# Which blocks are multiplied by seven products instead of eight, and in which order a pair's chunks run

## The chip, the core and the metric

The kernel runs on one core of one Trainium2 chip. The metric is the time of one execution on the device, in microseconds. Three runs of the kernel before took 2064.39, 2067.76 and 2068.39 us; the median, 2067.76 us, is the time before. The engines are called TensorE (PE in the profile), VectorE (DVE), ScalarE (ACT), GpSimd (POOL) and SyncE (SP, which issues the DMA transfers).

## The reference, cut to what matters

Two layers, each on 256 tokens of 2048 channels in float32. A layer normalises its input, multiplies it by one wide matrix, runs three kinds of attention on the result, and merges them:

```python
for l in range(DEPTH):
    h = rmsnorm(x, pre_norm_g[l])
    proj = jnp.einsum('bsd,dn->bsn', h, w_in[l])
    (qa, ka, va, qb, kb, vb, qc, kc, vc, za, zb, zc, gates) = jnp.split(proj, split_points, axis=-1)
    ya = neighbourhood_attention(...)              # branch A
    yb = gqa_attention(...)                        # branch B
    yc = dilated_mixture(...)                      # branch C
    ga, gb, gc = jnp.split(sigmoid(gates + b_gate[l]), 3, axis=-1)
    merged = (ga * ((ya * silu(za)) @ w_branch_a[l]) + gb * ((yb * silu(zb)) @ w_branch_b[l])
              + gc * ((yc * silu(zc)) @ w_branch_c[l]))
    x = x + rmsnorm(merged @ w_out[l], post_norm_g[l])
```

## The kernel before, in words

Nearly all the work is the product of the 256 tokens with streamed weights. Weights come in *blocks* of 512 output columns (`Blk`), and a block in *chunks* of 256 input channels, 512 KB each. One tile of a chunk holds two quarters, 128 input channels by 512 columns each. A chunk goes through four steps. SyncE issues its transfer (`emit_raw`). ScalarE rounds it to a high part (`emit_hi`, line 225). VectorE subtracts that from the weight for a low part (`emit_lo`, line 233). TensorE then makes, for each of the two quarters and each half T of the tokens, three matmuls of 512 columns (`mm3`, lines 188 to 190: high by high, low by high, high by low). A plain chunk is so 2 x 2 x 3 = 12 matmuls, a block of eight chunks 96.

The kernel writes out every engine's order by hand. `stream` lists the chunks, `order` says in which order TensorE works them, and before each step `ahead` emits the preparation of chunks further down the stream: transfers six chunks ahead, high parts three, low parts two. Near a pair (below) it looks further: transfers eight chunks ahead, low parts five, two at a time (`near`, lines 273 to 281). Each engine does its instructions strictly in the order of emission. After each chunk `slot` lets one or two steps of other work in: evacuations of finished blocks from PSUM (`evq`), attention heads (`heavy`), and *turns* (`tr_job`, `turn`). A turn rearranges tokens: VectorE transposes (line 166), SyncE sends the result to memory (line 171), and brings it back in another layout (line 175); ScalarE and VectorE then split it into high and low parts. SyncE issues in order too, so what is queued behind a turn's transfer waits with it.

Some blocks run as a *pair* (`two_blocks`). For the first two chunks of both blocks (a *unit* is one of these chunk pairs, `UNITS` is 2) seven block products stand for eight: with two token halves, two quarters and two blocks, each unit is a two-by-two block product, and the seven products of 128 x 128 x 512 are formed from sums and differences of its parts. The token sums come from `combos` (lines 477 to 491), once per layer for the layer's input (`CH`) and once for the merged tokens (`CM`). The weight differences are made for every unit by four subtractions of 128 x 512 on VectorE (lines 244 to 247, in the profile at line 237 of `minus`). A unit has parts A, B and C of two quarters each and shares a part D with the other unit, so the two units need seven tiles split where four plain chunks need four. The steps s1 to s6 issue the products (42 matmuls in all), interleaved with the first plain chunks; four sums of products are kept in SBUF (`total`, line 345), and one is added to each of the four accumulators when its block is evacuated (`whole`, line 397). From there the two blocks take turns by chunk: first block's chunk 3, second's 3, first's 4, and so on.

A layer's blocks come in this order: the gate path of branch C; its nine blocks of queries, keys and values (one plain, then four pairs); branch A, eight plain blocks; branch B, five; four *merges*; four output blocks. A merge has three gate blocks (the first two a pair), then the projections of A, C and B (four, two and four chunks); its result is turned and split (`mt_job`) for the output blocks, whose chunks 2 nb and 2 nb + 1 read the tokens of merge nb. The first two output blocks are a pair, the fourth works its token halves staggered (`lag`).

In the stretch of layer 0 of which the rows speak most: branch C's pairs start at 51.69, 104.06, 146.22 and 188.65 us, the plain blocks of A and B run from 234.99 to 544.54, the merges' gate pairs start at 544.54, 660.71, 755.99 and 847.87, and the output pair runs from 941.17 to 991.88. In layer 1 the merges and the output pair run from 1567.14 to 2016.19.

Of the kernel before, what the change touches and what calls it, by code (L numbers as in the profile page):

```python
# [30 lines left out]
UNITS = 2  # L31


class Blk:


    def __init__(self, w, nk, stat, evac, pre=None):
        self.w, self.nk, self.stat, self.evac, self.pre = w, nk, stat, evac, pre
        self.nc = nk // 2
        self.lag = False  # L40
        self.far = False
        self.twin = None
        self.twinned = False
        self.before = {}
        self.after = {}

# [18 lines left out]
def trunk(ctx, tc, x, xT, wpack, wbr_a, wbr_b, wbr_c, wout, pre_g, qk_g, bgate, post_g, abias,  # L65
# [127 lines left out]
    stream = []  # L193
    st = dict(raw=0, hi=0, lo=0, done=-1)
    RAW, HI, LO = {}, {}, {}
    order, ps = [], {}
# [109 lines left out]
    def two_blocks(one, two):  # L306

        units = [Unit(one, two, kc) for kc in range(UNITS)]
        head = units[0]
        head.all = units  # L310
        j = len(stream)
        for u in units:
            stream.extend([(u, "A"), (u, "B")])
        p1 = len(stream)
        stream.append((one, UNITS))
        stream.extend((u, "C") for u in units)
        d = len(stream)
        stream.append((head, "D"))
        rest = len(stream)
        stream.append((two, UNITS))  # L320
        for kc in range(UNITS + 1, one.nc):
            stream.extend([(one, kc), (two, kc)])
        bank, keep = {}, {}

        def plain(n, T):
            def f(u):
                h, lo, jj = one.stat(u.kc * 2 + n)
                c = slice(T * P, (T + 1) * P)
                return h[:, jj, c], lo[:, jj, c]
            return f  # L330

        def comb(n):
            def f(u):
                t = one.combos[u.kc]
                return t[:, 0, n], t[:, 1, n]
            return f

        def new(*names):
            for n in names:
                bank[n] = mm.tile([P, 512], F32, name="acc")  # L340
            ps.update({(blk, T): bank[n] for n, blk, T in
                       (("a", one, 0), ("d", one, 1), ("c", two, 0), ("w", two, 1)) if n in bank})

        def total(n, x, y):
            nc.vector.tensor_tensor(out=keep[n], in0=x, in1=y, op=ALU.add)  # L345

        def room():
            t = U("keep", [2, 512])
            return t[:, 0], t[:, 1]

        def s1():
            new("p1", "p5")
            product(bank["p1"], units, plain(0, 0), "A", 0, True)
            product(bank["p5"], units, comb(0), "B", 0, True)
            keep["c11"], keep["p16"] = room()
            nc.scalar.copy(keep["c11"], bank.pop("p1"))

        def s2():
            new("a")
            product(bank["a"], units, plain(1, 0), "A", 1, False)  # L360

        def s3():
            new("p6")
            product(bank["p6"], units, comb(1), "B", 1, True)
            total("p16", bank.pop("p6"), keep["c11"])
            for u in units:
                for x in "AB":
                    del u.h[x], u.lo[x]
            st["done"] = p1 - 1

        def s4():
            new("d")
            product(bank["d"], units, plain(1, 1), "C", 1, False)
            keep["c12"], keep["c21"] = room()
            total("c12", bank.pop("p5"), keep["p16"])

        def s5():
            new("p7")
            product(bank["p7"], units, comb(2), "C", 0, True)
            for u in units:  # L380
                del u.h["C"], u.lo["C"]
            st["done"] = d - 1

        def s6():
            new("c")
            product(bank["c"], units, comb(3), "D", 0, False)
            del head.h["D"], head.lo["D"]
            st["done"] = d
            total("c21", bank["p7"], keep["p16"])
            keep["c22"] = keep.pop("p16")  # L390
            total("c22", bank.pop("p7"), keep["c12"])
            new("w")

        def whole(evac, of):
            def f(T, x):
                k = keep.pop(of[T])
                nc.vector.tensor_tensor(out=x, in0=x, in1=k, op=ALU.add)  # L397
                yield from evac(T, x)
            return f

        one.evac, two.evac = whole(one.evac, ("c11", "c21")), whole(two.evac, ("c12", "c22"))

        order.extend([(p1 - 1, s1), (p1, s2), (p1, 0), (p1, s3), (d - 1, s4), (p1, 1), (d, s5), (d, s6),
                      (rest, 0), (rest + 1, 0), (rest, 1), (rest + 1, 1)])
        order.extend((i, T) for i in range(rest + 2, len(stream)) for T in range(2))


    prev = {}
# [1 line left out]
    def layer(l):  # L410
        blocks = []
# [81 lines left out]
        CH, CM = {}, {}  # L493

        def proj(nb, evac, pre=None):
            b = Blk([wpack[l, nb, kc] for kc in range(8)], 16, stat_h, evac, pre)
            b.combos = CH
            blocks.append(b)
            return b
# [277 lines left out]
        def merge(nb):  # L777
            G, BG = {}, {}

            def pre(i):  # L780
                def f():
                    BG[i] = work.tile([P, 512], F32, name="bg", bufs=3)
                    nc.sync.dma_start(out=BG[i], in_=bass.AP(
                        tensor=bgate.tensor, offset=bgate.offset + l * 6144 + i * 2048 + nb * 512,
                        ap=[[0, P], [1, 512]]))
                return f

            def evac_g(i):
                def f(T, ps):
                    if T == 0:  # L790
                        G[i] = U("g", [2, 512])
                    g = G[i][:, T]
                    nc.vector.scalar_tensor_tensor(g, ps, S["rs"][T], BG[i], op0=ALU.mult, op1=ALU.add)  # L793
                    nc.scalar.activation(g, g, AF.Tanh, scale=0.5)  # L794
                    yield
                return f

            def mt_job():

                MT[nb] = pair("mT", [4, 256])  # L800
                return tr_job(MT[nb], G[0])

            def evac_p(i):
                def f(T, ps):
                    nc.vector.scalar_tensor_tensor(G[i][:, T], G[i][:, T], 1.0, ps, op0=ALU.add, op1=ALU.mult)
                    if i:
                        nc.vector.tensor_tensor(out=G[0][:, T], in0=G[0][:, T], in1=G[i][:, T], op=ALU.add)
                    if i == 1 and T == 1:
                        later(mt_job())
                    yield  # L810
                return f

            gs = [proj(23 + 4 * i + nb, evac_g(i), pre=pre(i)) for i in range(3)]
            gs[0].pair(gs[1])
            for i, w, nk, ub in ((0, wbr_a, 8, (("a", 0), ("a", 1))), (2, wbr_c, 4, (("c", 0),)),
                                 (1, wbr_b, 8, (("b", 0), ("b", 1)))):
                blocks.append(Blk([w[l, nb, kc] for kc in range(nk // 2)], nk, stat_y(ub), evac_p(i)))
# [50 lines left out]
        second = cb[0]  # L868
        for k in (1, 3, 5, 7):
            cb[k].pair(cb[k + 1])  # L870
        for kc in range(UNITS):
            second.at("after", (6 + kc, 0), lambda kc=kc: CH.update({kc: combos(stat_h, kc)}))
        a_unit(0)
        a_unit(1)
        b0 = proj(20, evac_z(("b", 0)))
# [5 lines left out]
        for nb in range(4):  # L881
            merge(nb)
        outs = [out_block(nb) for nb in range(4)]
        outs[0].pair(outs[1])
        for kc in range(UNITS):
            blocks[-5].at("after", (1 + kc, 0), lambda kc=kc: CM.update({kc: combos(stat_m, kc)}))
        lastb = outs[3]
        lastb.lag = True

# [28 lines left out]
    for l in range(DEPTH):  # L918
        bl, S = layer(l)
        S0 = S0 or S  # L920
        for b in bl:
            i = len(stream)
            if b.twin:
                two_blocks(b, b.twin)
            elif not b.twinned:
                stream += [(b, kc) for kc in range(b.nc)]
                if b.lag:
                    a = [(i + k, 0) for k in range(b.nc)]
                    c = [(i + k, 1) for k in range(b.nc)]
                    order += a[:LAG]  # L930
                    for k in range(b.nc - LAG):
                        order += [a[LAG + k], c[k]]
                    order += c[b.nc - LAG:]
                else:
                    order += [(i + k, T) for k in range(b.nc) for T in range(2)]
# [3 lines left out]
    for i in range(8):  # L939
        nb, k = divmod(i, 2)  # L940
# [21 lines left out]
    for i, T in order:  # L962
        b, kc = stream[i]
# [119 lines left out]
```

## Time and profile before

| | us |
|---|---|
| median of three runs | 2067.76 (2064.39 to 2068.39) |
| the profiled execution: its own time | 2070.55 |
| the profiled execution: its span | 2068.2 |
| TensorE busy | 2006.3 (97%), 8990 matmuls |
| weight loads of TensorE | 1652.1 (80%) |
| VectorE busy | 1529.8 (74%) |
| ScalarE busy | 1066.4 (52%) |
| mean DMA rate | 226 GB/s |

The span runs from the first instruction of the program to the last; 2.35 us of the execution's own time lie around it. A busy share is the time in which an engine had an instruction running. Matmuls overlap, so the mean duration of one in a row (some 0.39 us) is longer than the time from one start to the next, and a busy TensorE may still be a slow one: the granted clock (PEclk) in a stretch's row tells at which of its two levels, 1.2 or 2.4 GHz, it ran, as a share of the higher.

### The profile page before, as it was taken

What the parts mean: (1) busy time and instruction counts of PE and PEld (TensorE: products, weight loads), DVE (VectorE), ACT (ScalarE), POOL (GpSimd) and SP (SyncE); (2) the same over time, 40 slices, a digit from 0 to 9 for tenths busy, and PEclk for the clock granted to TensorE, in tenths of its full rate; (3) what the DMA queues carried; (4) which work ended last, traced back from release to release, by engine and by line L of the source; (5) the groups of instructions that cost most, each with busy time, mean ns of one, the idle gap of its engine ahead of it and who ended that gap; (6) DMA issues with size and microseconds to landing.
All of it is one profiled execution on the core that took longest, in us unless ns stands there. A gap on an engine that the chain in (4) does not pass through costs nothing.

```text
span 2068.2 us, 24958 instructions
## 1 busy us (share of the span) xinstructions
PE 2006.3 (97%) x8990; PEld 1652.1 (80%) x8990; DVE 1529.8 (74%) x1973; ACT 1066.4 (52%) x1580; POOL 21.5 (1%) x31
## 2 busy tenths in 40 slices
PE   9899999999899999998999999999999999999988
PEld 7787888888677888787888878888887778787876
DVE  6888576768778676758688885876777786757675
ACT  6555465546555445444575554655555644444443
POOL 0000000000000000000000000000000000000000
PEclk9999999999999999999999999999999999999999
DMA  9556576756565647565756674858565657465643
GB/s 341 204 212 251 191 271 254 261 207 250 196 227 222 253 158 261 202 240 186 262 173 237 242 273 154 293 209 324 197 240 192 225 197 265 182 231 211 233 186 138
DMA packets 171724, 468.09 MB, mean 226 GB/s; under 512 B 15440, under 2 KB 58576, under 8 KB 171600
## 3 DMA queue, kind: packets, MB, share of 16 engines
q1 hardware_dynamic: 171600, 466.50, 61.9%
q8 instruction: 70, 1.15, 0.2%
q14 instruction: 54, 0.44, 0.1%
HBM read 427.11 MB, written 39.32 MB: 226 GB/s over the span
## 4 chain that ended last, share of the span: by engine, by line
PE 75%; DVE 13%; DMA 5%; ACT 3%; issue 3%; SPq 0%; DVEq 0%; POOL 0%; ACTq 0%; POOLq 0%
PE acc L189 24%; PE acc L188 24%; PE acc L190 24%; DVE wl L233 3%; DMA raw<-in_wpack_dram 2%; DVE wl L237 2%; DVE tt L166 1%; DMA tx<-turn 1%; DVE ta L237 1%; DVE tb L237 1%; DMA turn<-tt 1%; ACT wh L225 1%; DMA x<-in_x_dram 1%; DVE acc L397 0%; DVE keep L345 0%
## 5 line engine op out<-in xcount | busy, mean ns | idle before, releaser
L189 PE MATMUL acc<-wl,hTh 128*128 128x512 f32 x2080 | 816.5, 393 | 22.4 <-DVE wl L233 11.5
L188 PE MATMUL acc<-wh,hTh 128*128 128x512 f32 x2080 | 817.4, 393 | 3.0 <-DVE s L721 2.7
L190 PE MATMUL acc<-wh,hTl 128*128 128x512 f32 x2080 | 813.7, 391 | 0.0
L233 DVE TENSOR_TENSOR wl<-raw,wh 128x1024 fp32r<-128x1024 f32 (+1 forms) x634 | 751.3, 1212 | 65.3 <-ACT wh L225 63.9
L225 ACT CAST wh<-raw 128x1024 fp32r<-128x1024 f32 (+1 forms) x634 | 633.6, 1041 | 171.8 <-DMA raw<-in_wpack_dram 98.8
L189 PEld LDWEIGHTS acc<-wl,hTh 128*128 128x128 f32 x2080 | 393.2, 189 | 111.4 <-DVE wl L233 16.9
L188 PEld LDWEIGHTS acc<-wh,hTh 128*128 128x128 f32 x2080 | 393.2, 189 | 85.3 <-issue 3.5
L190 PEld LDWEIGHTS acc<-wh,hTl 128*128 128x128 f32 x2080 | 392.8, 189 | 82.3
L189 PE MATMUL acc<-wl,yTh 128*128 128x512 f32 x320 | 124.8, 390 | 1.2 <-DVE wl L233 1.2
L188 PE MATMUL acc<-wh,yTh 128*128 128x512 f32 x320 | 124.6, 389 | 0.0
L190 PE MATMUL acc<-wh,yTl 128*128 128x512 f32 x320 | 124.5, 389 | 0.0
L397 DVE TENSOR_TENSOR acc<-acc,keep 128x512 f32<-128x512 f32 x72 | 49.8, 692 | 74.9 <-PE acc L190 74.9
L794 ACT ACTIVATE g<-g 128x512 f32<-128x512 f32 x48 | 30.4, 633 | 140.1 <-DVE g L793 140.1
L189 PE MATMUL acc<-wl,mTh 128*128 128x512 f32 x236 | 93.2, 395 | 7.1 <-DVE wl L237 7.1
L257 ACT CAST wh<-ta 128x1024 fp32r<-128x1024 f32 x36 | 37.9, 1053 | 120.3 <-DVE ta L237 117.5
L569 ACT ACTIVATE sp<-sp,nm 128x256 f32<-128x256 f32 (+1 forms) x48 | 27.6, 577 | 131.0 <-DVE nm L564 131.0
L188 PE MATMUL acc<-wh,mTh 128*128 128x512 f32 x236 | 93.6, 397 | 0.0
L190 PE MATMUL acc<-wh,mTl 128*128 128x512 f32 x236 | 92.9, 394 | 0.0
L188 PE MATMUL acc<-wh,cs 128*128 128x512 f32 x144 | 59.9, 416 | 17.6 <-ACT cs L147 10.4
L166 DVE STREAM_TRANSPOSE tt<-tok 128x512 f32<-128x512 f32 (+1 forms) x72 | 72.8, 1049 | 0.0
L793 DVE SCALAR_TENSOR_TENSOR g<-acc,rsx,bg 128x512 f32<-128x512 f32 x48 | 36.0, 749 | 49.2 <-PE acc L190 48.1
L189 PEld LDWEIGHTS acc<-wl,yTh 128*128 128x128 f32 x320 | 60.1, 188 | 14.2 <-DVE wl L233 2.0
(137 smaller groups left out, 1864.9 us busy)
## 6 DMA issues: line engine op xcount, KB each, us to landing
raw<-in_wpack_dram SPq DMA_DIRECT2D x558, 512.0 KB, 6.0
raw<-in_wo_dram SPq DMA_DIRECT2D x64, 512.0 KB, 7.5
turn<-tt SPq DMA_DIRECT2D x50, 512.0 KB, 3.0
tx<-turn SPq DMA_DIRECT2D x50, 512.0 KB, 5.8
raw<-in_wa_dram SPq DMA_DIRECT2D x32, 512.0 KB, 4.3
raw<-in_wb_dram SPq DMA_DIRECT2D x32, 512.0 KB, 3.9
turn<-tt SPq DMA_DIRECT2D x34, 256.0 KB, 2.2
tx<-turn SPq DMA_DIRECT2D x34, 256.0 KB, 4.5
```

The source lines that it names most:

```text
L166: nc.vector.transpose(out=tt[:, :, T].rearrange("p j (h a) -> p h j a", h=n), in_=srcs[T].rearrange("p (h b j) -> p h j b", h=n, j=4))
L188: nc.tensor.matmul(out_, lhsT=lh, rhs=rh, start=first, stop=False)
L189: nc.tensor.matmul(out_, lhsT=lh, rhs=rl, start=False, stop=False)
L190: nc.tensor.matmul(out_, lhsT=ll, rhs=rh, start=False, stop=last)
L225: nc.scalar.copy(HI[i][:, k], RAW[i][:, k])
L233: nc.vector.tensor_tensor(out=LO[i][:, k], in0=RAW[i][:, k], in1=f32(HI[i][:, k]), op=ALU.subtract)
L237: nc.vector.tensor_tensor(out=out_, in0=a, in1=b, op=ALU.subtract)
L257: nc.scalar.copy(u.h[what], RAW[u, what])
L397: nc.vector.tensor_tensor(out=x, in0=x, in1=k, op=ALU.add)
L569: nc.scalar.activation(p[:, i], sc[:, i], AF.Exp, bias=nm[:, i:i + 1], scale=1.0 if f is None else f[:, i:i + 1], accum_out=sm[:, i:i + 1])
L793: nc.vector.scalar_tensor_tensor(g, ps, S["rs"][T], BG[i], op0=ALU.mult, op1=ALU.add)
L794: nc.scalar.activation(g, g, AF.Tanh, scale=0.5)
```

## The change

Three things are edited.

- The merges' gate blocks and the output blocks are no longer pairs; all three gate blocks of a merge run as plain blocks. The four pairs of branch C in each layer stay. The first two output blocks become *mates*: six chunks of the first, six of the second, then the last two of the first and the last two of the second. The token sums of the merged tokens (`CM`) go.
- In a pair that stays, the first block's chunk 3 is put ahead of part D, both token halves of it before s6, and after that the first block's chunks 4 to 7 run before the second's 3 to 7. So the first block's last chunk stands five chunks ahead of the second's (one before). A flag `late` that would run their last two chunks otherwise is never set.
- The two token sums of the layer's input are emitted behind chunks 3 and 4 of the block ahead of the first pair, instead of chunks 6 and 7.

```diff
@@ two_blocks
         stream.append((one, UNITS))
         stream.extend((u, "C") for u in units)
-        d = len(stream)
-        stream.append((head, "D"))
+        mid = len(stream)
+        stream.extend([(one, UNITS + 1), (head, "D")])
+        d = mid + 1
         rest = len(stream)
         stream.append((two, UNITS))
-        for kc in range(UNITS + 1, one.nc):
-            stream.extend([(one, kc), (two, kc)])
+
+        ones, twos = list(range(UNITS + 2, one.nc)), list(range(UNITS + 1, two.nc))
+        if one.late:
+            stream.extend([(one, kc) for kc in ones[:-2]] + [(two, kc) for kc in twos[:-2]])
+            ones, twos = ones[-2:], twos[-2:]
+        stream.extend([(one, kc) for kc in ones] + [(two, kc) for kc in twos])
...
-            st["done"] = d - 1
+            st["done"] = mid - 1
...
-        order.extend([(p1 - 1, s1), (p1, s2), (p1, 0), (p1, s3), (d - 1, s4), (p1, 1), (d, s5), (d, s6),
-                      (rest, 0), (rest + 1, 0), (rest, 1), (rest + 1, 1)])
-        order.extend((i, T) for i in range(rest + 2, len(stream)) for T in range(2))
+        order.extend([(p1 - 1, s1), (p1, s2), (p1, 0), (p1, s3), (mid - 1, s4), (p1, 1), (mid - 1, s5),
+                      (mid, 0), (mid, 1), (d, s6)])
+        order.extend((i, T) for i in range(rest, len(stream)) for T in range(2))
@@ merge
-            gs = [proj(23 + 4 * i + nb, evac_g(i), pre=pre(i)) for i in range(3)]
-            gs[0].pair(gs[1])
+            [proj(23 + 4 * i + nb, evac_g(i), pre=pre(i)) for i in range(3)]
@@ layer
         for kc in range(UNITS):
-            second.at("after", (6 + kc, 0), lambda kc=kc: CH.update({kc: combos(stat_h, kc)}))
+            second.at("after", (3 + kc, 1), lambda kc=kc: CH.update({kc: combos(stat_h, kc)}))
...
-        outs[0].pair(outs[1])
-        for kc in range(UNITS):
-            blocks[-5].at("after", (1 + kc, 0), lambda kc=kc: CM.update({kc: combos(stat_m, kc)}))
+        outs[0].mate, outs[1].mated = outs[1], True
@@ trunk
-            elif not b.twinned:
+            elif b.mate:
+                m = b.mate
+                stream += [(b, kc) for kc in range(6)] + [(m, kc) for kc in range(6)]
+                stream += [(c, kc) for c in (b, m) for kc in range(6, 8)]
+                order += [(k, T) for k in range(i, len(stream)) for T in range(2)]
+            elif not b.twinned and not b.mated:
```

## Rows read from the trace of the kernel before

**Rows 1.** The page: its span, and busy us (share of the span) and instructions of each engine

```profile
span 2068.2 us, 24958 instructions
...
PE 2006.3 (97%) x8990; PEld 1652.1 (80%) x8990; DVE 1529.8 (74%) x1973; ACT 1066.4 (52%) x1580; POOL 21.5 (1%) x31
```

**Rows 2.** Busy us of each engine by stretch; x: instructions; PEclk: granted TensorE clock

```profile
core 0: us, PE busy (x) PEld busy (x) DVE busy (x) ACT busy (x) POOL busy (x), PEclk, DMA share, GB/s
104.06:146.22 42.16, 42.16 (x188) 34.92 (x186) 33.79 (x39) 21.71 (x27) 0.00 (x0) 1.00 0.67 249
234.99:544.54 309.55, 309.55 (x1470) 260.03 (x1468) 226.61 (x314) 172.11 (x290) 6.25 (x8) 1.00 0.65 239
544.54:991.88 447.34, 427.36 (x1880) 349.62 (x1878) 331.09 (x422) 211.15 (x291) 2.02 (x2) 0.98 0.59 215
1567.14:2016.19 449.05, 430.03 (x1879) 351.32 (x1878) 330.96 (x421) 210.80 (x291) 2.02 (x2) 0.98 0.60 214
544.54:602.13 57.59, 51.36 (x229) 40.60 (x228) 45.50 (x78) 31.43 (x69) 2.02 (x2) 0.97 0.60 206
602.13:631.13 29.00, 25.69 (x127) 21.52 (x126) 22.21 (x39) 18.18 (x36) 0.00 (x0) 1.00 0.59 209
660.71:707.03 46.32, 44.08 (x187) 35.99 (x186) 34.73 (x39) 20.87 (x24) 0.00 (x0) 0.96 0.64 238
941.17:991.88 50.71, 45.10 (x188) 36.43 (x186) 37.67 (x46) 21.45 (x26) 0.00 (x0) 0.93 0.49 182
188.65:234.99 46.34, 44.07 (x188) 35.98 (x187) 30.39 (x34) 22.97 (x28) 0.00 (x0) 0.96 0.62 227
1210.62:1257.13 46.51, 43.95 (x187) 35.90 (x186) 30.69 (x35) 22.96 (x28) 0.00 (x0) 0.96 0.62 229
51.69:104.06 52.37, 45.99 (x188) 36.80 (x186) 44.79 (x58) 26.62 (x34) 0.00 (x0) 0.90 0.54 202
```

**Rows 3.** What PE waited for, 544.54 to 991.88 us: total, times, longest

```profile
PE acc L189 <- DVE wl L237: 9.2, 7, 3.5
PE acc L189 <- DVE wl L233: 5.5, 4, 3.3
```

**Rows 4.** PE's timeline, start of the second merge's pair: start us, duration us, instruction

```profile
661.39 0.39 PE L188 MATMUL acc<-wh,hTh 128*128 128x512 f32 x1
664.02 0.67 PE L189 MATMUL acc<-wl,hTh 128*128 128x512 f32 x1 [2.24 <-DVE wl L237]
```

**Rows 5.** Busy time in the stretch just behind that wait

```profile
664.50:667.40 2.90, 2.90 (x8) 2.31 (x7) 2.87 (x4) 1.49 (x3) 0.00 (x0) 0.50 0.06 21
```

**Rows 6.** DVE's groups by line and shape: count | busy us, mean ns | idle before

```profile
L397 DVE TENSOR_TENSOR acc<-acc,keep 128x512 f32<-128x512 f32 x72 | 49.8, 692 | 74.9 <-PE acc L190 74.9
L345 DVE TENSOR_TENSOR keep<-acc,keep 128x512 f32<-128x512 f32 x72 | 49.3, 684 | 0.6
L237 DVE TENSOR_TENSOR wl<-ta,wh 128x1024 fp32r<-128x1024 f32 x36 | 43.8, 1218 | 1.2 <-ACT wh L257 1.2
...
L237 DVE TENSOR_TENSOR ta<-raw 128x512 f32<-128x512 f32 x36 | 24.7, 685 | 3.2 <-DMA raw<-in_wpack_dram 3.1
```

**Rows 7.** PE's timeline in layer 0's last branch C pair

```profile
201.96 0.50 PE L188 MATMUL acc<-wh,cs 128*128 128x512 f32 x1 [2.27 <-DVE keep L345]
```

**Rows 8.** DVE's timeline beside it

```profile
201.23 0.67 DVE L345 TENSOR_TENSOR keep<-acc,keep 128x512 f32<-128x512 f32 x1
```

**Rows 9.** DVE's timeline ahead of the first pair

```profile
38.94 1.23 DVE L233 TENSOR_TENSOR wl<-raw,wh 128x1024 fp32r<-128x1024 f32 x1 [1.09 <-ACT wh L225]
...
56.87 0.68 DVE L554 SCALAR_TENSOR_TENSOR tok<-tok,acc 128x512 f32<-128x512 f32 x1
57.46 1.22 DVE L233 TENSOR_TENSOR wl<-raw,wh 128x1024 fp32r<-128x1024 f32 x1
```

**Rows 10.** SP's own waits, 235 to 544 us, ahead of a turn's transfer

```profile
SPq L171 <- DVE tt L166: 174.8, 22, 15.3
```

**Rows 11.** SP's own waits, 941 to 992 us, ahead of a turn's transfer

```profile
SPq L171 <- DVE tt L166: 23.0, 1, 23.0
```

More of the change, by code (lines that the diff above doesn't have):

```diff
@@ L42, in __init__ @@
         self.twin = None
-        self.twinned = False
+        self.twinned = self.late = self.mated = False
+        self.mate = None
         self.before = {}
```

## The prediction

> **What bounds the kernel now.** I read the busy shares first, then busy time by stretch, then TensorE's waits, then the timelines at the longest of them. The shares make TensorE the bound: 2006.3 of 2068.2 us [rows 1]. So work added there should cost, and the question is what its time is made of.
>
> An undisturbed pair shows the price of a matmul. In 104.06 to 146.22 a seven-product pair issues 186 weight matmuls (42 for products, 12 chunks of 12) in 42.16 us without a gap: 0.2267 us each [rows 2]. The attention stretch, 234.99 to 544.54, holds thirteen plain blocks, 1248 weight matmuls or 282.9 us, and some 221 smaller matmuls in the other 26.6, 0.12 us each. TensorE is busy through all of its 309.55 us there, with VectorE busy for 226.61, 73% [rows 2]. Plain blocks beside heavy head work thus lose nothing.
>
> The stretches from the first merge to the end of the output pair are different. Each holds five of the ten pairs that the change dissolves: 5 x 186 + 4 x 216 = 1794 weight matmuls (406.7 us) and about 85 smaller ones (10.2), 416.9 us of issue. They last 447.34 and 449.05 [rows 2]. So 30.4 and 32.1 us, together 62.5, are lost, of which the table's idle time shows only a part. The rest is clock. TensorE waits for a difference of a prepared unit: at 664.02 a matmul starts 2.63 us after the last instead of 0.23 [rows 4], and right behind it the granted clock is 0.50, that is 1.2 GHz, with eight matmuls in 2.90 us [rows 5]. The wait of 2.24 costs 4.2 us in its pair (46.32 less 42.16) [rows 2].
>
> Where it lies, layer 0: first merge's pair 57.59 less 42.16 and 43 small ones at 0.12, 10.3; the third gate block behind it 29.00 less 21.76 and 31 small ones, 3.5; second merge 4.2; output pair 50.71 less 42.16, 8.6 [rows 2]. The remaining 3.8 are in merges three and four and the last projection of the first. The waits named most are units' differences (9.2 us, line 237) and plain chunks' (5.5, line 233) [rows 3], both VectorE's: it is late although busy for only 331.09 of 447.34 us [rows 2].
>
> **The change part by part.** I add the terms to the profiled execution, 2070.55 us with 2.35 outside its span; the median of the runs shown, 2067.76, lies 2.8 lower.
>
> (a) Products. Ten pairs (four merges and one output pair in each of two layers) go from 42 to 48 matmuls over their first two chunk pairs: 60 x 0.2267 = **+13.6 us**, all on TensorE, which has no cover for it.
>
> The Trainium skill, "TensorE: Matmul & The Clock Gate", section "Back-to-back issue gap", gives N/2.4 + 2.5 ns for a matmul on its own, 215.7 ns at 512 columns, and about 131 ns sustained. By those the sixty would be an estimated 12.9 or 7.9 us; this trace's 226.7 ns decides.
>
> (b) What the pairs cost VectorE. Each drops four differences of a chunk's quarters per unit, eight at 0.69; four totals at 0.68; four additions ahead of evacuation at 0.69; and its units need seven tiles split instead of the plain four, three more at 1.22 [rows 6]. That is 5.5 + 2.7 + 2.8 + 3.7 = 14.7 us per pair, 147 in ten, much of it bunched ahead of the pair's first matmul, plus the output pairs' token sums. ScalarE drops three casts and a copy per pair. Each five-pair stretch would then keep about 331 - 74 = 257 us of VectorE work over 423.7 us, 61%, under the 73% at which the attention stretch lost nothing. In the first merge's three gate blocks it is 45.50 + 22.21 - 14.7 = 53 over some 74, 72%, just that level [rows 2].
>
> So I let the 62.5 us go, but not quite: in the first merge the rotary evacuation of the block before now meets head jobs, in a plain block whose split runs two chunks ahead rather than five. From the attention stretch that costs 0; from the third gate block's 3.5 (a plain-chunk wait) up to 3.5 per layer, or below nothing by no more than rounding since the issue floor holds. I take 1.5 per layer, nearer the attention stretch because of its VectorE share. **-59.5**.
>
> The output pair's new order needs the last merge's turned tokens twelve chunks in, 32.6 us; its job emits the turned split after its sixth chunk. Beginning with six chunks of the first block needs only the three earlier merges' tokens. I cost it at nothing; the cover is those six chunks, 16.3 us, and if the turn were later than that the excess would be a wait.
>
> (c) Branch C's order. The fourth product (D) moves behind both halves of a plain chunk: 12 matmuls, 2.72 us. In the last pair of each layer D waits 2.27 us [rows 7] for the first total, which ends at 201.9 [rows 8]; the two pairs lose 46.34 and 46.51 less 42.16, 4.2 and 4.35 [rows 2]. D would now come at 199.5 + 2.72 = 202.2. The block that ends earlier (four chunks sooner; its partner's end is five chunks behind it) also takes two evacuation additions out of VectorE's queue at the next pair's start, 1.4 us. The chunk moved ahead of D needs its split 1.2 us earlier than D's; it takes D's place in the same queue of six. The second block's other half is no longer interleaved, but starts 1.36 us later than before. Bounds: 0 (the wait moves to that chunk) and 8.55; with both shifts pointing one way I take **-8.4**. The other pairs lose nothing today.
>
> (d) Token sums three chunks earlier. Layer 0's first pair loses 52.37 - 42.16 = 10.2 [rows 2]. VectorE works there without rest from the first units on, so sums put ahead only delay the units behind them. What they gain: the two instructions that today stand before the last sum, the gate path's 0.68 and a plain chunk's 1.22 [rows 9], no longer hold up the first products, and some of the 1.09 us gaps ahead of each split [rows 9] are filled; with fewer half-clock matmuls after a shorter wait I take **-3.5**, between +1 (the last chunk before the pair is now late) and -10.2. Layer 1's first pair has VectorE far ahead; nothing there.
>
> Sum: +13.6 - 59.5 - 8.4 - 3.5 = **-57.8**: 2070.55 would be 2012.8, and 2067.76 gives **2010 us**.
>
> **Rivals.**
> 1. VectorE stays late in the first merge. Then its 10.3 + 3.5 stay in both layers, 24.6 more than the 3 that I left: 2035. For it: evacuations with rotary and heads fall together. Against: same VectorE share as a stretch that loses nothing, and the pair's bunch gone.
> 2. TensorE's work alone counts: the waits belong to VectorE's general lag and come back at other instructions. Then +13.6 meets only (c) and (d), -11.9: 2069, no change. For it: 97% busy. Against: the plain blocks between the pairs. The Trainium skill, "Perfetto Trace Analysis", section "Identifying the Most-Contended Engine", says to optimise first the engine with the highest occupancy, and to judge TensorE by its weight loads; by that rule, adding to TensorE is the wrong way. The weight-load share of 80% shows room, so the trace only half agrees.
> 3. Slower: SP's queue. The merged tokens' turn holds SP until VectorE has transposed; in the output pair that was 23.0 us [rows 11], and weights behind it are not issued. Pairs look eight chunks ahead for transfers, plain blocks six, 16.3 us. Were SP held as long, each of eight starts (merges two to four, the output pair, two layers) would lose 6.7 plus some 1.7 of half clock [rows 5], 67 us against 62.5 - 13.6 + 11.9 = 60.8 gained: 2074. It decides from 7.6 us per start. Against: SP was held up to 15.3 us under the same six chunks in the attention stretch [rows 10], without loss, and VectorE's bunch, which made the 23.0, goes.
> 4. All lost time goes, the first pair's included: 48.9 + 8.6 + 10.2 = 67.7, 2000.
>
> **How the numbers follow.** Forecast (2003 to 2022) 0.76, rival 1 in whole 0.10, rival 2 0.02, rival 3 0.03, rival 4 0.09. The range 2000 to 2030 takes in the bounds of (b) to (d) and half of rival 1. A difference under about 0.2%, 4 us, is no change here: faster 0.95, same 0.02, slower 0.03.
>
> **What would show it.** The two stretches should last about 425 us each, with TensorE's gaps under 2 us and granted clock 1.00; the last branch C pairs 42.2; the first pair some 49, its wait now for a unit's difference and not for a sum. VectorE's busy time should fall by about 155 us, TensorE's count rise by 60. Rival 1 would leave waits for line 233 in the first merge, rival 2 waits spread over the plain blocks, rival 3 ScalarE waiting for transfers with TensorE idle behind it. The prediction is wrong if the two stretches stay above 437.

## The result and the profile after

The changed kernel takes 2017.21 us (median of 4, 2014.5 to 2018.05) against 2068.07 beside it: ratio 0.9753, 95% interval 0.9734 to 0.9771, so 50.9 us faster. The forecast was 2010 within 2000 to 2030. The profiled execution took 2016.78 us, with a span of 2014.7; the steps below are compared by spans, 53.5 us apart.

The page of the changed kernel: span, and busy time by engine [rows 1].

```profile
span 2014.7 us, 24751 instructions
...
PE 1994.3 (99%) x9050; PEld 1651.9 (82%) x9050; DVE 1387.9 (69%) x1749; ACT 1029.2 (51%) x1526; POOL 21.4 (1%) x31
```

Sixty matmuls more, TensorE busy for 12.0 us less: some of what was shown as busy before was matmuls at half clock. The rows below go by stretch (columns as in [rows 2]): first the two from the first merge to the end of the output pair, then the first merge's first gate block and its other two, the second merge's three, the output mates, the last branch C pairs of both layers, layer 0's first pair.

```profile
536.35:963.34 426.99, 424.97 (x1910) 352.09 (x1908) 264.22 (x317) 194.23 (x266) 2.01 (x2) 1.00 0.64 224
1535.98:1962.71 426.73, 424.87 (x1909) 352.07 (x1908) 264.30 (x317) 193.82 (x266) 2.01 (x2) 1.00 0.63 224
536.35:563.74 27.39, 25.57 (x122) 20.66 (x121) 20.76 (x37) 15.32 (x38) 2.01 (x2) 1.00 0.54 192
563.74:613.70 49.96, 49.76 (x243) 41.71 (x241) 37.48 (x66) 32.25 (x61) 0.00 (x0) 1.00 0.66 230
642.38:707.66 65.28, 65.28 (x290) 54.05 (x288) 36.17 (x37) 22.10 (x26) 0.00 (x0) 1.00 0.68 244
919.82:963.34 43.52, 43.52 (x194) 36.04 (x192) 24.60 (x26) 14.47 (x20) 0.00 (x0) 1.00 0.66 244
184.58:226.76 42.18, 42.18 (x187) 34.88 (x186) 29.04 (x32) 20.15 (x26) 0.00 (x0) 1.00 0.73 249
1182.36:1225.72 43.36, 42.50 (x188) 34.83 (x187) 30.24 (x33) 21.33 (x27) 0.00 (x0) 1.00 0.72 251
51.69:99.56 47.87, 44.09 (x188) 35.92 (x186) 42.96 (x50) 27.45 (x34) 0.00 (x0) 0.96 0.60 218
```

The stretches shrink by 20.35 and 22.32 us, the last branch C pairs by 4.16 and 3.15, the first pair by 4.5: 54.5, of which 1.0 is given back in small waits of other blocks. The second merge and the output mates run without any gap at 0.2267 us a matmul (65.28 for 288, 43.52 for 192). What TensorE still waits for in layer 0's stretch is one kind of thing [rows 3]:

```profile
PE acc L190 <- DVE wl L234: 2.0, 3, 1.1
```

All three are in the first merge: the low part of a plain chunk comes late. VectorE's timeline there says why (start us, duration, what; in brackets the idle time before and what ended it):

```profile
538.42 0.23 DVE L739 TENSOR_SCALAR hss<-hss,rsx 128x4 f32<-128x4 f32 x1 [2.56 <-ACT junk L737]
...
544.28 0.23 DVE L739 TENSOR_SCALAR hss<-hss,rsx 128x4 f32<-128x4 f32 x1 [2.10 <-ACT junk L737]
...
545.02 1.22 DVE L234 TENSOR_TENSOR wl<-raw,wh 128x1024 fp32r<-128x1024 f32 x1
```

VectorE stands still for 2.56 and 2.10 us in the rotary evacuation, because ScalarE has not finished the squares that it needs. The split queued behind the second of these ends at 546.24, and TensorE, which waits 1.14 us for it, goes on at 546.29.

### The profile page after: what moved, and what is told of

It is laid out like the page before. It is cut to its first block, busy times and chain, and to the rows that moved or that the text cites. A ratio compares the mean times of both kernels' runs of the same rounds, so it can differ in the third digit from the quotient of the medians.

```text
span 2014.7 us, 24751 instructions
## 1 busy us (share of the span) xinstructions
PE 1994.3 (99%) x9050; PEld 1651.9 (82%) x9050; DVE 1387.9 (69%) x1749; ACT 1029.2 (51%) x1526; POOL 21.4 (1%) x31
## 4 chain that ended last, share of the span: by engine, by line
PE 88%; DVE 5%; ACT 3%; DMA 2%; issue 1%; SPq 0%; DVEq 0%; POOL 0%; POOLq 0%; ACTq 0%
PE acc L190 28%; PE acc L191 28%; PE acc L189 28%; DMA raw<-in_wpack_dram 2%; DVE wl L234 1%; ACT wh L226 1%; DVE tt L167 1%; DMA tx<-turn 1%; ACT sp L575 1%; DVE nm L570 0%; ACT sp L586 0%; PE sc L191 0%; PE o L191 0%; PE o L190 0%; PE sc L652 0%
## 5 line engine op out<-in xcount | busy, mean ns | idle before, releaser
L190 PE MATMUL acc<-wl,hTh 128*128 128x512 f32 x2160 | 843.4, 390 | 10.2 <-DVE wl L234 5.2
L189 PE MATMUL acc<-wh,hTh 128*128 128x512 f32 x2160 | 844.7, 391 | 0.0
L234 DVE TENSOR_TENSOR wl<-raw,wh 128x1024 fp32r<-128x1024 f32 (+1 forms) x674 | 799.9, 1214 | 64.4 <-ACT wh L226 64.2
L191 PE MATMUL acc<-wh,hTl 128*128 128x512 f32 x2160 | 841.3, 390 | 0.0
L226 ACT CAST wh<-raw 128x1024 fp32r<-128x1024 f32 (+1 forms) x674 | 676.4, 1042 | 274.1 <-DMA raw<-in_wpack_dram 160.3
L191 PEld LDWEIGHTS acc<-wh,hTl 128*128 128x128 f32 x2160 | 405.6, 188 | 84.4
L189 PEld LDWEIGHTS acc<-wh,hTh 128*128 128x128 f32 x2160 | 406.1, 188 | 83.4 <-ACT wh L226 1.2
L800 ACT ACTIVATE g<-g 128x512 f32<-128x512 f32 x48 | 30.4, 634 | 177.3 <-DVE g L799 177.3
L811 DVE SCALAR_TENSOR_TENSOR g<-g,acc 128x512 f32<-128x512 f32 x48 | 32.8, 684 | 61.2 <-PE acc L191 61.1
L191 PEld LDWEIGHTS acc<-wh,yTl 128*128 128x128 f32 x320 | 60.1, 188 | 12.5
L189 PEld LDWEIGHTS acc<-wh,yTh 128*128 128x128 f32 x320 | 60.1, 188 | 12.4
```

Source lines behind the costliest of these rows:

```text
L189: nc.tensor.matmul(out_, lhsT=lh, rhs=rh, start=first, stop=False)
L190: nc.tensor.matmul(out_, lhsT=lh, rhs=rl, start=False, stop=False)
L191: nc.tensor.matmul(out_, lhsT=ll, rhs=rh, start=False, stop=last)
L226: nc.scalar.copy(HI[i][:, k], RAW[i][:, k])
L234: nc.vector.tensor_tensor(out=LO[i][:, k], in0=RAW[i][:, k], in1=f32(HI[i][:, k]), op=ALU.subtract)
```

## The experiments

The theory is that a pair lost its time because VectorE's preparation for it came in one bunch, ahead of the first product and with little lead (the time from a piece of preparation to its use), while over a whole merge VectorE has room. The first rival is that the order of the chunks and the evacuations at a pair's start were the cause. The second is VectorE's total load. In the code cuts `...` marks what is left out.

**The pairs put back, in the new order.**

```diff
+            gs = [proj(23 + 4 * i + nb, evac_g(i), pre=pre(i)) for i in range(3)]
+            gs[0].pair(gs[1])
...
-        outs[0].mate, outs[1].mated = outs[1], True
+        outs[0].pair(outs[1])
+        outs[0].late = True
+        for kc in range(UNITS):
+            blocks[-5].at("after", (1 + kc, 0), lambda kc=kc: CM.update({kc: combos(stat_m, kc)}))
```

> The ten pairs of the merges and the output blocks are put back, in the new chunk order (the output pair with its flag late, so that it reads the last merge's tokens no sooner than before); the two other edits stay. Theory (what was lost lay in the pairs' own preparation on VectorE): sixty matmuls fewer, 13.6 us, but the waits for line 237's differences come back; the two stretches from the first merge to the end of the output pair last 435 to 447 us each instead of 427, the time 2035 to 2058 us. Rival (the chunk order and the evacuations ahead of the next pair were the cause): the waits stay away, the stretches last 417 to 421 us, the time 2004 to 2010.

2057.16 us (2056.38 to 2058.79), ratio to the kernel before 0.9942 (0.9926 to 0.9958). Its two stretches, the first merge's pair, the second merge's in either layer, the fourth merge's and the output pair:

```profile
538.04:984.84 446.80, 429.40 (x1879) 352.15 (x1878) 333.05 (x424) 212.55 (x293) 2.02 (x2) 0.98 0.61 215
1556.17:2002.21 446.04, 428.85 (x1879) 351.76 (x1878) 332.13 (x423) 212.25 (x293) 2.02 (x2) 0.98 0.61 215
538.04:599.49 61.45, 53.53 (x230) 42.96 (x228) 47.55 (x82) 32.12 (x71) 2.02 (x2) 0.92 0.54 193
655.93:702.22 46.29, 44.05 (x187) 35.98 (x186) 36.17 (x41) 21.61 (x25) 0.00 (x0) 0.96 0.65 238
1675.01:1719.75 44.74, 42.49 (x187) 34.84 (x186) 36.16 (x41) 21.60 (x25) 0.00 (x0) 1.00 0.66 246
843.04:885.91 42.87, 42.45 (x187) 34.84 (x186) 34.35 (x39) 20.09 (x24) 0.00 (x0) 1.00 0.72 262
934.87:984.84 49.97, 45.33 (x187) 36.46 (x186) 38.76 (x48) 22.56 (x28) 0.00 (x0) 0.93 0.50 192
```

The stretches are nearly back at what they were [rows 2], so the first rival falls: under the new order, dissolving the pairs is worth 19.8 and 19.3 us, 39.1 of the 42.7. The other 3.6 are the distance of this run's stretches from those of the kernel before, 0.5 and 3.0 us, from one profile each. The rows also show that not every pair lost more than it saved. In merges three and four it now loses 0.7 us (42.87 less 42.16; 42.87 to 42.90 in both layers), less than the 1.36 that its seven products save.

**VectorE's work given back, spread out and in a bunch.** Twelve idle subtractions of 128x1024 for each former pair (`extra(n)`), spread behind six chunks of each of its two blocks, or all in front. The spread version is shown whole for the merges; the output blocks have the same.

```diff
+            for b in gs[:2]:
+                for kc in (0, 1, 2, 4, 5, 6):
+                    b.at("after", (kc, 1), lambda: extra(1))
...
+            gs[0].at("before", (0, 0), lambda: extra(12))      # the bunch, instead
```

> As the changed kernel, with idle work on VectorE of about what a pair cost it: twelve subtractions of 128x1024 in the two blocks of each former pair (14.6 us, 146 in all), one behind each of six chunks of a block. Theory (the pairs lost by the bunch, not by the amount): nothing in merges two to four and the output blocks, 0 to 4 us in each first merge; 2017 to 2026 us. Rival (VectorE's total load is what counts): most of the 50 us comes back, 2045 us or more.

> The same twelve subtractions, all in front of the first chunk of each former pair. Theory of the bunch: the plain chunks' split is only two chunks ahead, 5.4 us, so each of ten bunches leaves TensorE waiting some 8 to 10 us and at half clock for 1.7 us after: 2100 to 2135 us. Rival of the amount: the same time as with the work spread out.

Spread: 2033.47 us, ratio 0.983 (0.9811 to 0.985); in a bunch: 2150.03, one run. Both are above what the theory had expected. The spread version's stretch from the first merge to the end of the output mates, then its first merge (three gate blocks), second merge's gate blocks, output mates, and layer 1's first merge:

```profile
537.23:972.67 435.44, 428.48 (x1910) 354.34 (x1908) 331.41 (x377) 193.76 (x266) 2.01 (x2) 0.99 0.63 219
537.23:622.82 85.59, 78.63 (x362) 64.69 (x361) 72.88 (x116) 47.53 (x98) 2.01 (x2) 0.96 0.58 197
651.50:716.78 65.28, 65.28 (x290) 54.05 (x289) 49.60 (x49) 22.10 (x26) 0.00 (x0) 1.00 0.68 245
929.15:972.67 43.52, 43.52 (x194) 36.04 (x192) 38.22 (x38) 14.47 (x20) 0.00 (x0) 1.00 0.64 240
1545.19:1629.20 84.01, 77.64 (x361) 63.40 (x360) 71.47 (x114) 47.55 (x98) 2.01 (x2) 0.98 0.59 200
```

The bunch in the second merge's first gate block, and TensorE's timeline at its chunk 2:

```profile
657.45:692.15 34.70, 24.10 (x97) 19.42 (x96) 27.89 (x27) 4.10 (x5) 0.00 (x0) 0.85 0.37 129
```

```profile
673.88 0.79 PE L192 MATMUL acc<-wl,hTh 128*128 128x512 f32 x1 [10.60 <-DVE wl L236]
674.47 0.63 PE L193 MATMUL acc<-wh,hTl 128*128 128x512 f32 x1
```

With the work spread out VectorE is busy for 331.41 us of layer 0's stretch, as in the kernel before (331.09 [rows 2]), and yet the stretch loses 11.7 us (435.44 less the 423.7 of its matmuls) and not 30.4. In merges two to four and the output blocks the spread work costs nothing, with VectorE busy for up to 38.22 of 43.52 us, 88%; the bunch costs 12.9 us in the second merge's first gate block (34.70 less 21.76), a wait of 10.6 and the half clock behind it (0.63 us a matmul instead of 0.39). It is the same work, so there it is the bunch. This bunch met a split two chunks ahead and a pair's met one five ahead, so the run shows that a bunch costs, not how much it cost the pairs. In the first merge the amount counts as well: 85.59 and 84.01 us against 77.35 (27.39 + 49.96) in layer 0 and 77.1 in layer 1. So 15.1 of the 16.3 us are lost there, where I had expected 0 to 8. The second rival holds in this one place, and it is not a small one: of the 10.5 us that the change regains in layer 0's first merge (13.8 before, 3.3 after), the amount alone takes 8.2 away again.

**Branch C's order taken apart.** The whole old order; then only the move of D kept, the blocks alternating after it:

```diff
-        ones, twos = list(range(UNITS + 2, one.nc)), list(range(UNITS + 1, two.nc))
...
-        stream.extend([(one, kc) for kc in ones] + [(two, kc) for kc in twos])
+        for kc in range(UNITS + 1, one.nc):
+            if kc > UNITS + 1:
+                stream.append((one, kc))
+            stream.append((two, kc))
```

> As the changed kernel, with the pairs of branch C in the old chunk order (D right behind C, the two blocks alternating). Theory: the last pair of branch C in each layer loses its 4.2 and 4.3 us again, D waiting 2.3 us for the first total (46.3 us each instead of 42.2 and 43.4); about 2024 us. Rival (the shorter waits there came from the earlier token sums, or from chance): no difference, 2017.

> As the changed kernel, but of branch C's new order only the move of D behind a plain chunk is kept; after it the two blocks alternate again. Theory (both shifts help, the 2.72 us ahead of D by themselves suffice): the last pairs of branch C 42.2 to 43.4 us as with the whole change, their wait for the first total gone. Rival (the earlier end of the first block and its evacuations is what does it): D still waits, 44 us or more. About 2017 us by the theory, 2021 by the rival.

Old order: 2022.14 us; D alone: 2015.34. The last branch C pairs in the old order, and D's wait in layer 0; then the same pairs with D alone:

```profile
186.76:231.36 44.60, 42.45 (x188) 34.83 (x187) 30.29 (x34) 22.98 (x28) 0.00 (x0) 1.00 0.66 247
1186.76:1230.97 44.21, 42.44 (x187) 34.83 (x186) 29.89 (x33) 22.88 (x28) 0.00 (x0) 1.00 0.67 250
```

```profile
199.94 0.50 PE L189 MATMUL acc<-wh,cs 128*128 128x512 f32 x1 [2.15 <-DVE keep L346]
```

```profile
183.86:226.04 42.18, 42.18 (x187) 34.91 (x186) 30.42 (x34) 23.07 (x28) 0.00 (x0) 1.00 0.70 259
1181.73:1223.89 42.16, 42.16 (x188) 34.92 (x187) 28.36 (x31) 21.27 (x26) 0.00 (x0) 1.00 0.71 260
```

D's wait returns in the old order, 2.15 us in layer 0 and 1.77 in layer 1, but costs 2.4 and 2.05 us, not 4.2 and 4.3 (with waits of 2.27 [rows 7] and 2.56): here no half clock followed it, the granted clock being 1.00 in both rows. The move of D alone takes all of it away, in layer 1 better than the whole change (42.16 against 43.36). So the earlier end of the first block, which I had counted as help, is not needed for D. In the whole change the 1.2 us of layer 1 stand at a wait of 0.86 for a unit's difference (line 238) at the pair's start. Whether the earlier end of the first block causes it is not shown, with one run of each.

**The token sums at their old place.**

```diff
-            second.at("after", (3 + kc, 1), lambda kc=kc: CH.update({kc: combos(stat_h, kc)}))
+            second.at("after", (6 + kc, 0), lambda kc=kc: CH.update({kc: combos(stat_h, kc)}))
```

> As the changed kernel, with the token sums at their old place. Theory: layer 0's first pair waits for the sums again and lasts 51 to 53 us instead of 47.9; nothing else moves; about 2021 us. Rival (the gain in that pair came from the chunk order): 48 to 49 us, no change.

2020.94 us, one run. Layer 0's first pair, and what TensorE waits for from 51 to 104 us:

```profile
51.98:103.69 51.71, 45.77 (x187) 36.73 (x186) 43.28 (x57) 26.44 (x33) 0.00 (x0) 0.90 0.56 203
```

```profile
PE acc L189 <- ACT cs L148: 5.9, 2, 3.2
```

With the sums early the same stretch of the changed kernel has a single wait, for a unit's difference:

```profile
PE acc L190 <- DVE wl L238: 3.8, 1, 3.8
```

Earlier sums are worth 3.8 us (51.71 less 47.87): two waits for `cs`, the token sums rounded by ScalarE, become one for a unit's difference.

**No mates.** The output blocks one after the other (the mates' line taken out).

> As the changed kernel, with the output blocks one after the other. Theory (the six chunks of the second block cover the last merge's turn): the first output block's chunk 6 waits for the turned tokens, 4 to 7 us in each layer with the half clock behind it; 2025 to 2031 us. Rival (the turn is in time anyway): 2017.

2028.58 us, one run. The first output block in both layers, its 96 matmuls by themselves taking 21.76, and TensorE at its chunk 6 in layer 0:

```profile
920.24:948.99 28.75, 24.90 (x98) 20.00 (x96) 14.29 (x16) 5.25 (x8) 0.00 (x0) 0.88 0.77 278
1926.89:1952.71 25.82, 23.95 (x98) 18.99 (x96) 14.30 (x16) 5.25 (x8) 0.00 (x0) 0.93 0.75 263
```

```profile
940.57 0.80 PE L189 MATMUL acc<-wh,mTh 128*128 128x512 f32 x1 [3.85 <-ACT mTh L148]
```

The last merge's tokens come about 20 us after the block's start, so six chunks (16.3 us) don't cover their turn and the mates' twelve (32.6 us) do.

**Versions put together from this.** The first has layer 0's first pair dissolved (its token sums go to the block behind), the pairs of merges three and four put back, and a split five chunks ahead in the first merge's first gate block and the block ahead of it:

```diff
-        la, room = (8, 13) if b.far else (0, 6)
+        la, room = (8, 13) if b.far else (b.la, 6 + b.la)
...
+            if nb in (2, 3):
+                gs[0].pair(gs[1])
+            if nb == 0:
+                gs[0].la = blocks[-4].la = 5
...
-        for k in (1, 3, 5, 7):
+        for k in (1, 3, 5, 7)[l == 0:]:
```

> A version put together from what the runs showed: layer 0's first pair dissolved too (5.7 us lost in it against 1.36 saved: -4.3), the pairs of merges three and four put back (0.7 lost against 1.36 saved: -2.7 over four), and in the first merge's first gate block and the block ahead of it the split runs five chunks ahead as near a pair (about 2.5 us lost per layer there: -3 to -5). Theory: 2004 to 2008 us. Rival (waits move elsewhere): 2012 or more.

2004.42 us (2003.69 to 2006.94), ratio 0.9689 (0.9673 to 0.9705). The first merge's gate blocks take 74.78 instead of 77.35:

```profile
530.53:605.31 74.78, 74.36 (x362) 62.67 (x360) 55.07 (x99) 44.80 (x95) 2.02 (x2) 1.00 0.61 213
```

Then comes the test of the theory that matters most: give the pairs more lead instead of dissolving them (merges two to four; D's move alone), and in the last version the output pair too, its token sums emitted in the last merge's third gate block instead of its last projection. The edits against the version above, D's order left out:

```diff
-LA_UNIT, NEAR = 5, 4
+LA_UNIT, NEAR = 7, 6
...
-            if nb in (2, 3):
+            if nb in (1, 2, 3):
...
-        outs[0].mate, outs[1].mated = outs[1], True
+        outs[0].pair(outs[1])
+        for kc in range(UNITS):
+            blocks[-8].at("after", (2 + 2 * kc, 0), lambda kc=kc: CM.update({kc: combos(stat_m, kc)}))
```

> As the version of the run before it (layer 0's first pair dissolved, longer lookahead in the first merge), with the pairs of merges two to four, of branch C's new order only the move of D, and near a pair the split up to seven chunks ahead instead of five, begun six chunks ahead instead of four. Theory (a pair loses by the bunch of its preparation, and VectorE has room for it if it comes earlier): the six pairs of merges two to four take 42.2 us each, 1.36 less than plain blocks; 1998 to 2002 us. Rival (VectorE can't fit the pairs' work in at all): their waits stay at 0.6 to 2.5 us with the half clock, 2004 us or more.

> The same with the output pair put back, its token sums emitted in the last merge's third gate block. Theory of the bunch: 42.2 us for the output pair too, 1.4 us less per layer; 1995 to 2000 us. Rival: the output pair waits for line 237's differences again, as its start also has the last merge's evacuations; 2004 us or more.

Without the output pair 2002.77 us (2002.1 to 2003.54), ratio 0.968 (0.9664 to 0.9696), a little over the theory's range; with it 1998.45 us (1998.28 to 1999.49), ratio 0.9661 (0.9647 to 0.9676), the fastest of all. The intervals of these three ratios overlap, so it is the rows that tell the steps apart. In the last version, the second merge's pair, the third's, and the output pair of layer 0:

```profile
634.37:678.97 44.60, 42.89 (x187) 34.68 (x186) 35.43 (x40) 20.70 (x24) 0.00 (x0) 1.00 0.72 255
727.93:770.09 42.16, 42.16 (x187) 34.91 (x186) 31.24 (x35) 18.82 (x21) 0.00 (x0) 1.00 0.71 252
910.17:952.33 42.16, 42.16 (x187) 34.91 (x186) 30.43 (x34) 16.10 (x20) 0.00 (x0) 1.00 0.61 229
```

With more lead the pairs of merges three and four run at the price of their matmuls, 42.16 us, where they lost 0.7 each with the pairs put back (in the whole new order there, with D's move alone here). The output pair, which lost 8.6 us before [rows 2], does so too, but two things had changed for it. VectorE's timeline shows both, first with the pairs put back (the pair starts at 934.87), then in the last version (910.17): the first weight difference, a token sum, and the last split that the pair's first products need.

```profile
926.62 0.69 DVE L238 TENSOR_TENSOR ta<-raw 128x512 f32<-128x512 f32 x1
931.43 0.68 DVE L489 TENSOR_TENSOR cf<-mTh,mTl 128x512 f32<-128x512 f32 x1
939.34 1.22 DVE L238 TENSOR_TENSOR wl<-ta,wh 128x1024 fp32r<-128x1024 f32 x1
```

```profile
897.30 0.68 DVE L240 TENSOR_TENSOR ta<-raw 128x512 f32<-128x512 f32 x1
908.23 1.22 DVE L240 TENSOR_TENSOR wl<-ta,wh 128x1024 fp32r<-128x1024 f32 x1
```

The differences begin 12.9 us ahead of the pair instead of 8.2, and the token sum that stood among them for 3.1 us is gone from there; the split ends 0.7 us before the pair instead of 5.7 behind its start. What the lead alone would have done for this pair was not run. The second merge's pair still loses 2.4 us, with a wait of 1.5, although its preparation runs up to seven chunks ahead. With the same 44.60 us it made the version without the output pair miss its range. The 2.4 are more than the 1.36 that the pair saves, so it should stay plain; this last step was not run, and neither was the first merge's pair with more lead.

## Why the prediction was right, point by point

- *What bounds the kernel.* Right. In layer 0's stretch idle time fell from 19.98 us (447.34 less 427.36) to 2.02; the other 10.4 of the 30.4 us lost before lay inside the busy share, most of it half clock by the granted clock of 0.98 over the stretch [rows 2], and 1.3 of it is left.
- *(a) +13.6.* Right: 9050 matmuls, and the plain merges run at the price used.
- *(b) -59.5.* The direction and place right, the size 3.3 us too large. The lost time is 3.3 and 3.0 us per layer (426.99 and 426.73 less 423.7), not 1.5; in layer 0 it is the rotary evacuation meeting head jobs, as said, near the upper bound of 3.5. VectorE's share there was a poor guide twice over: it came out at 58.2 of 77.35 us (20.76 + 37.48), 75% and not 72%, and it does not count the 2.56 and 2.10 us in which VectorE waits in order for ScalarE. The term was forecast whole from the stretch's lost time, with a bunch as the reason; by the spread run the amount of VectorE's work, without any bunch, stands for 15.1 of the 56.2 us regained, all in the first merges. VectorE's busy time fell by 142 us, not 155: I added durations, and consecutive instructions overlap (the four differences of a unit by up to some 0.08 us).
- *(c) -8.4.* The two profiles give 7.3, but the experiment gives less: with the old order put back the two pairs take 88.8 us against 85.5, 3.3 more, and 4.5 more than with D's move alone. Most of the rest of the 7.3 was half clock behind D's wait, which followed in the kernel before and not in that run (one run each), so part of the agreement is luck. The mechanism, D's wait for the first total, is right and D's move alone removes it; that the earlier end of the first block helps as well was wrong.
- *(d) -3.5.* 4.5 between the two profiles, 3.8 by the experiment, for the reason given.
- *The rest.* 1.0 us of small waits in branch C's middle pairs and one block of branch B was not forecast. Terms and rest make 53.5 against the forecast's 57.8; the medians are 50.9 apart.
- *Output order.* It was costed at nothing. Right: the mates run at 43.52 us without a gap, and without them the two first output blocks lose 7.0 and 4.1 us.
- *Rivals.* 1 (VectorE stays late in the first merge) holds for 3 of its 14 us per layer. 2 (TensorE's work alone) falls with the result and the first experiment. By the rule of the Trainium skill, "Perfetto Trace Analysis", section "Identifying the Most-Contended Engine", the engine with the highest occupancy comes first; here that engine, TensorE, got 60 matmuls more and the time fell, so occupancy by itself did not point to the change. The Trainium skill, "Perfetto Trace Analysis", section "Optimization Strategy", says to look at the gaps within a regime and to make what they wait for start sooner; the last version agrees, at 1998.45 us. 3 (SP's queue) cost nothing, but not for the reason given: the hold behind the last merge's turn did not go with the bunch. It was still 20.7 us (the row below, 900 to 990 us), longer than the 16.3 of six chunks, and TensorE ran through it and through the mates without a gap. The time of 4, 2000, was reached by the last version through other edits, not by the change.

```profile
SPq L172 <- DVE tt L167: 20.7, 1, 20.7
```

## What to carry to other kernels

An algorithm that saves work on the busy engine and pays on another is judged where the payment falls. Bunched ahead of its first use it can cost several times the saving, as the output pair did (8.6 us against 1.36). The same work spread out cost nothing where the other engine had room, and 15.1 us in the two first merges, where it had not; begun two chunks earlier it cost nothing in merges three and four and still 2.4 us in the second. Price a stretch by its undisturbed cost per instruction and compare: at a busy share of 97% two stretches had lost 62.5 us, 23.5 of them inside the busy time. Before taking a fast algorithm out, try giving it lead.

## What the runs showed of the hardware that was not expected

The half clock behind a wait does not follow from the wait's length alone. With the pairs put back, a wait of 2.24 us in layer 0's second merge was followed by a granted clock of 0.50, one of 2.25 us at the same instruction in layer 1 by 1.00; the pair took 46.29 and 44.74 us. The two stretches just behind, layer 1's first:

```profile
1678.90:1681.50 2.60, 2.60 (x13) 2.11 (x12) 2.56 (x4) 1.84 (x4) 0.00 (x0) 1.00 0.00 0
659.70:662.50 2.80, 2.80 (x9) 2.12 (x8) 2.77 (x4) 1.42 (x2) 0.00 (x0) 0.50 0.05 13
```

So a wait of that size was worth 2.6 or 4.1 us here, and two stretches of the same code differ by 1.5 us. What decides between the two was not tried.
